# Softmax over rows of 512: one in-place ring, the row maximum, and small chunks at both ends

## Chip, cores, metric

The kernel runs on one core of one Trainium2 chip. The metric is device time in microseconds (us) of one execution. Before: 163.57 us, median of 3 runs (163.49 to 163.68).

## The reference

```python
x = np.random.randn(16, 1024, 512).astype(np.float32)

def reference(x):
    x_max = np.max(x, axis=-1, keepdims=True)
    exp_x = np.exp(x - x_max)
    return (exp_x / np.sum(exp_x, axis=-1, keepdims=True)).astype(np.float32)
```

There are 16384 rows of 512 numbers, 33.55 MB in and 33.55 MB out. Spread over 128 partitions, that is 128 rows of 2 KB for each partition. In what follows "a row" means one row in every partition: 128 rows must be loaded and 128 stored.

## The kernel before

Sixteen chunks of 8 rows. Loads go out from SyncE's queue, stores from ScalarE's (ACT's). Input and output have separate tiles. The maximum is off: with numbers drawn from a normal distribution the exponentials do not overflow.

```python
R, XBUFS, EBUFS = 8, 7, 4
for t in range(nchunks):                                   # 16
    x_tile = x_pool.tile([P, R, d], F32)                   # 7 buffers
    nc.sync.dma_start(out=x_tile, in_=x_t[t])
    nc.gpsimd.tensor_copy(out=guard_tile, in_=x_tile[:, 0, 0:1])
    # ... use_max is off: no reduce_max ...
    e_tile = e_pool.tile([P, R, d], F32)                   # 4 buffers
    for r in range(R):
        nc.scalar.activation(out=e_tile[:, r, :], in_=x_tile[:, r, :], func=Exp,
                             bias=0.0, scale=1.0, accum_out=sums[:, r : r + 1])
    nc.vector.reciprocal(out=recip, in_=sums)
    nc.vector.tensor_mul(out=e_tile, in0=e_tile, in1=recip_b)   # 128x4096, recip broadcast
    nc.scalar.dma_start(out=out_t[t], in_=e_tile)
# ... four memsets on GpSimd at the end ...
```

The softmax here doesn't subtract the row's maximum and nothing guards it: scores larger than these inputs give would overflow.

Of the kernel before, what the change touches and what calls it, by code (L numbers as in the profile page):

```python
# [2 lines left out]

# [4 lines left out]


@with_exitstack  # L10
def kernel(
    ctx: ExitStack,
    tc: tile.TileContext,
    x: bass.AP,
    out: bass.AP,
):
    nc = tc.nc
    P = nc.NUM_PARTITIONS

    x_flat = x.flatten_outer_dims()  # L20
    out_flat = out.flatten_outer_dims()
    n, d = x_flat.shape

    R = int(os.environ.get("SM_R", "8"))
    XBUFS = int(os.environ.get("SM_XBUFS", "7"))
    EBUFS = int(os.environ.get("SM_EBUFS", "4"))

    rows_per_chunk = P * R
    assert n % rows_per_chunk == 0
    nchunks = n // rows_per_chunk  # L30

    x_t = x_flat.rearrange("(t p r) d -> t p r d", p=P, r=R)
    out_t = out_flat.rearrange("(t p r) d -> t p r d", p=P, r=R)

    x_pool = ctx.enter_context(tc.tile_pool(name="xp", bufs=XBUFS))
    e_pool = ctx.enter_context(tc.tile_pool(name="ep", bufs=EBUFS))
    stats_pool = ctx.enter_context(tc.tile_pool(name="stats", bufs=12))
    guard_pool = ctx.enter_context(tc.tile_pool(name="guard", bufs=1))

    use_max = os.environ.get("SM_USEMAX", "0") == "1"  # L40

    guard_tile = guard_pool.tile([P, 1], mybir.dt.float32)

    e_tiles = []
    for t in range(nchunks):
        x_tile = x_pool.tile([P, R, d], mybir.dt.float32)
        nc.sync.dma_start(out=x_tile, in_=x_t[t])  # L47

        nc.gpsimd.tensor_copy(out=guard_tile, in_=x_tile[:, 0, 0:1])  # L49

        if use_max:
            neg_max = stats_pool.tile([P, R], mybir.dt.float32)
            nc.vector.reduce_max(
                out=neg_max, in_=x_tile, axis=mybir.AxisListType.X, negate=True
            )

        e_tile = e_pool.tile([P, R, d], mybir.dt.float32)
        e_tiles.append(e_tile)
        sums = stats_pool.tile([P, R], mybir.dt.float32)
        for r in range(R):  # L60
            nc.scalar.activation(  # L61
                out=e_tile[:, r, :],
                in_=x_tile[:, r, :],
                func=mybir.ActivationFunctionType.Exp,
                bias=neg_max[:, r : r + 1] if use_max else 0.0,
                scale=1.0,
                accum_out=sums[:, r : r + 1],
            )

        recip = stats_pool.tile([P, R], mybir.dt.float32)  # L70
        nc.vector.reciprocal(out=recip, in_=sums)  # L71

        recip_b = recip.unsqueeze(2).to_broadcast([P, R, d])
        nc.vector.tensor_mul(out=e_tile, in0=e_tile, in1=recip_b)  # L74

        nc.scalar.dma_start(out=out_t[t], in_=e_tile)  # L76

    for b in range(min(EBUFS, nchunks)):
        e_tile = e_tiles[nchunks - 1 - b]
        nc.gpsimd.memset(e_tile[:, 0, 0:1], 0.0)  # L80


# [1 line left out]
_INS = ['x']  # L84
_OUTS = [((16, 1024, 512), 'float32')]


# [23 lines left out]
```

## Time and profile before

| | before |
|---|---|
| median | 163.57 us |
| span of the profiled run | 161.6 us |
| DVE (VectorE) busy | 74.0 us |
| ACT (ScalarE) busy | 80.8 us |
| transfers | 67.1 MB, 415 GB/s over the span |

These lines are from the page of the kernel before. The rows of 40 digits cut the span into 40 equal slices (4.0 us each); a digit is the busy share of its slice in tenths, 9 being 90% or more. A costliest-group line reads: line, engine, operation, output from input, shapes, count, then busy us and mean ns of one, then idle time just before. POOL is GpSimd.

```profile
span 161.6 us, 456 instructions
...
DVE 74.0 (46%) x32; ACT 80.8 (50%) x257; POOL 18.5 (11%) x24
...
DVE  0006970994196419082000008941992499069600
ACT  3089519924893481900000199339906970995000
...
DMA  5999999999999999999999999999999999999993
GB/s 150 434 434 426 434 373 422 432 430 430 438 426 426 446 422 426 450 422 426 446 410 442 438 418 438 434 422 440 426 430 442 418 434 442 418 434 442 418 434 146
...
L61 ACT ACTIVATE e_tile<-x_tile 128x512 f32<-128x512 f32 x128 | 78.5, 615 | 66.1 <-DMA x_tile<-in_x_dram 35.1
L74 DVE TENSOR_TENSOR e_tile<-e_tile,recip 128x4096 f32<-128x4096 f32 x16 | 70.8, 4425 | 0.5
```

The DMA row is the one to read first: nine in every slice but the first and the last. No engine is busy for more than half of the span. So the kernel is bound by its transfers, and it can only gain where the row is not 9.

The same as a table of stretches (start and end in us, length, busy us of each engine with its count, clock, DMA share, GB/s):

```profile
core 0: us, DVE busy (x) ACT busy (x) POOL busy (x), PEclk, DMA share, GB/s
...
30.00:100.00 70.00, 28.92 (x13) 31.09 (x101) 9.92 (x8) 1.00 1.01 431
...
112.00:140.00 28.00, 18.51 (x8) 17.69 (x57) 4.82 (x3) 1.00 1.01 430
140.00:161.00 21.00, 9.25 (x4) 7.57 (x26) 0.40 (x4) 1.00 0.91 389
```

The Trainium skill, "DMA: Bandwidth & Descriptors", section "Where 436 GB/s comes from", gives 16 ports of 32 bytes at 850 MHz as the ceiling, 435 GB/s. The trace agrees: 431 and 430 GB/s over long stretches (single slices swing to both sides of that).

The last links of the chain that ended last (start us, length us, what):

```profile
147.84 4.43 DVE e_tile L74
...
152.35 8.28 DMA out_dram<-e_tile
```

A store of 2 MB alone takes 4.9 us at this rate. This one took 8.28 us from issue to landing, because one more store was still ahead of it.

### The profile page before, as it was taken

Reading aid. Unit: us, or ns where it says so; the run is one execution under the profiler, and the core shown is the slowest. Engines: PE = TensorE matmul, PEld = TensorE weight load, DVE = VectorE, ACT = ScalarE, POOL = GpSimd, SP = SyncE. Lnnn points to the kernel's source line nnn. Section 1 sums busy time; section 2 is a strip of 40 time slices with the busy share of each in tenths; the row PEclk is TensorE's granted clock in tenths of the full one; section 3 lists DMA queues with packets and bytes.
Section 4 is the critical chain, followed back from the end, with each engine's and each line's share of the span. In section 5 each row is a group of like instructions: output and inputs, shape, how many; then the busy total and the mean of one; then the engine's idle time right before and its main releaser. Section 6 shows DMA issues by size and latency. Waiting matters only on the chain.

```text
span 161.6 us, 456 instructions
## 1 busy us (share of the span) xinstructions
DVE 74.0 (46%) x32; ACT 80.8 (50%) x257; POOL 18.5 (11%) x24
## 2 busy tenths in 40 slices
DVE  0006970994196419082000008941992499069600
ACT  3089519924893481900000199339906970995000
POOL 0000000034090001000000006200082000000000
DMA  5999999999999999999999999999999999999993
GB/s 150 434 434 426 434 373 422 432 430 430 438 426 426 446 422 426 450 422 426 446 410 442 438 418 438 434 422 440 426 430 442 418 434 442 418 434 442 418 434 146
DMA packets 4610, 67.13 MB, mean 415 GB/s; under 512 B 512, under 2 KB 512, under 8 KB 512
## 3 DMA queue, kind: packets, MB, share of 16 engines
q1 hardware_dynamic: 2304, 33.56, 49.4%
q10 hardware_dynamic: 2304, 33.56, 48.5%
q14 instruction: 2, 0.02, 0.0%
HBM read 33.55 MB, written 33.55 MB: 415 GB/s over the span
## 4 chain that ended last, share of the span: by engine, by line
DMA 52%; ACT 28%; DVE 17%; issue 1%; ACTq 1%; POOLq 0%; SPq 0%
DMA x_tile<-in_x_dram 35%; ACT e_tile L61 28%; DMA out_dram<-e_tile 17%; DVE e_tile L74 16%; DVE recip L71 1%; ACTq L76 1%; POOLq L106 0%; POOLq L80 0%; SPq L47 0%
## 5 line engine op out<-in xcount | busy, mean ns | idle before, releaser
L61 ACT ACTIVATE e_tile<-x_tile 128x512 f32<-128x512 f32 x128 | 78.5, 615 | 66.1 <-DMA x_tile<-in_x_dram 35.1
L74 DVE TENSOR_TENSOR e_tile<-e_tile,recip 128x4096 f32<-128x4096 f32 x16 | 70.8, 4425 | 0.5
L71 DVE RECIPROCAL recip<-sums 128x8 f32<-128x8 f32 x16 | 3.2, 203 | 77.7 <-ACT e_tile L61 77.7
L49 POOL COPY guard_tile<-x_tile 128x1 f32<-128x1 f32 x16 | 17.9, 1116 | 119.0 <-DMA x_tile<-in_x_dram 119.0
L61 ACT ACTIVATION_READ_ACCUMULATOR e_tile<-x_tile 128x1 f32 x128 | 23.9, 187 | 0.0
L80 POOL MEMSET e_tile<- 128x1 f32 x4 | 0.4, 99 | 23.1 <-DMA out_dram<-e_tile 23.1
L61 ACT ACT_TABLE_LOAD x1 | 1.3, 1283 | 0.7 <-PEq L95 0.7
L95 POOL MEMSET const-float32-0.0<- 128x1 f32 x1 | 0.1, 99 | 0.2 <-issue 0.2
L95 POOL MEMSET const-uint8-127<- 128x1 uint8 x1 | 0.1, 103 | 0.0
L95 POOL MEMSET const-bfloat16-1.0<- 128x1 bf16 x1 | 0.1, 102 | 0.0
L95 POOL MEMSET const-float32-1.0<- 128x1 f32 x1 | 0.1, 99 | 0.0
## 6 DMA issues: line engine op xcount, KB each, us to landing
x_tile<-in_x_dram SPq DMA_DIRECT2D x16, 2048.0 KB, 42.2
out_dram<-e_tile ACTq DMA_DIRECT2D x16, 2048.0 KB, 18.2
```

What stands on the lines that cost most here:

```text
L49: nc.gpsimd.tensor_copy(out=guard_tile, in_=x_tile[:, 0, 0:1])
L61: nc.scalar.activation(out=e_tile[:, r, :], in_=x_tile[:, r, :], func=mybir.ActivationFunctionType.Exp, bias=neg_max[:, r : r + 1] if use_ ...
L71: nc.vector.reciprocal(out=recip, in_=sums)
L74: nc.vector.tensor_mul(out=e_tile, in0=e_tile, in1=recip_b)
L76: nc.scalar.dma_start(out=out_t[t], in_=e_tile)
L80: nc.gpsimd.memset(e_tile[:, 0, 0:1], 0.0)
L95: nc = _bacc.Bacc("TRN2", target_bir_lowering=False, num_devices=1)
```

## The change

It does four things at once: it adds the row maximum; it computes in place, in one ring of eleven 8-row buffers; it multiplies row by row with a per-partition scalar; and it makes the first and the last chunks small, so that compute starts earlier and the last chain is short. (GpSimd's guard copies and its last memsets go too.) The core of it:

```diff
+CHUNKS = [1, 1, 2, 4] + [8] * 14 + [4, 2, 1, 1]
+SLOTS = {1: 2, 2: 1, 4: 1, 8: 11}
 # ... (views by chunk, pools: cut)
+    def load(k):
+        tiles[k] = data.tile([P, R, d], F32, name=f"x{R}", tag=f"x{R}", bufs=SLOTS[R])
+        nc.sync.dma_start(out=tiles[k], in_=src[k])
+    def rowmax(k):
+        nc.vector.reduce_max(out=shift[k], in_=tiles[k], axis=AX, negate=True)
+    def exps(k):
-                out=e_tile[:, r, :],
-                in_=x_tile[:, r, :],
+                out=tiles[k][:, r, :],
+                in_=tiles[k][:, r, :],
-                bias=neg_max[:, r : r + 1] if use_max else 0.0,
+                bias=shift[k][:, r : r + 1],
+    def scale(k):
-        nc.vector.tensor_mul(out=e_tile, in0=e_tile, in1=recip_b)
+        for r in range(R):
+            nc.vector.tensor_scalar_mul(out=tiles[k][:, r, :], in0=tiles[k][:, r, :],
+                                        scalar1=recip[:, r : r + 1])
+    def store(k):
+        nc.scalar.dma_start(out=dst[k], in_=tiles[k])
+    with tc.manual_schedule():
+        for k in range(K):
+            load(k); rowmax(k); exps(k)
+            if k >= 1:
+                scale(k - 1); store(k - 1)
+        scale(K - 1); store(K - 1)
```

The store of chunk k-1 stands on ACT's queue behind the exponentials of chunk k. Chunks are counted from 0 below, so chunks 4 to 17 have 8 rows.

## The prediction

> **What bounds it now.** The transfers. The page shows the DMA engines at nine tenths or more in 38 of 40 slices, at 410 to 450 GB/s; DVE is busy 46% and ACT 50%. The windows view gives 432 GB/s for 30-96 us and 413 for 136-160. The Trainium skill, "DMA: Bandwidth & Descriptors", section "Where 436 GB/s comes from", puts the ceiling at 435 GB/s; this trace agrees (434 at best). 67.1 MB at 430 GB/s are 156 us of the 161.6 us span. The chain of waits names ACT and DVE for long stretches (28% and 17%), but they only kept pace with the queues: the last store was issued at 152.35 us and landed 8.28 us later, though 2 MB need 4.9, so stores were queued to the end.
>
> **What the change does.** No byte is saved. Nothing large can be won.
> - Maximum: DVE gains one reduction over every element. The multiply of 128x4096 takes 4425 ns today; the skill's "VectorE: DVE Perf Modes", section "The perf-mode tier table", has tensor_reduce at 1x like the fp32 tensor_tensor, so I estimate 4.4 us per 8 rows. It gives fp32 tensor_scalar 2x: 8 operations of about 0.33 to 0.42 us, 2.6 to 3.4 us in place of 4.4. With the reciprocal an 8-row chunk costs DVE some 7.3 to 8.1 us, 117 to 131 us in all. Below the 9.7 us that loading and storing a chunk take together, but above the 4.9 us of storing alone.
> - ACT: the same 128 exps of 613 ns, now in place, about 79 us; POOL's guards go.
> - Small end chunks start compute near 4 us instead of 8.5 and shorten the last chain, but DMA is already full in both places. 32 transfers become 44, a few with 2 KB pieces: estimate 0 to 1 us.
> - The ring is ample, yet in the listing of the built kernel the transfers still share eight completion semaphores. The store of the twelfth chunk waits until the load five chunks later has landed, and the next waits for the load after that. They stand on ACT's queue, so exps stop too. Loads then run alone for about 15 us and several stores are left for the end, where DVE's 7.3 to 8.1 us per chunk is slower than the stores' 4.9. I estimate 1 to 4 us of DMA idle near 140-155 us.
>
> **Sum.** 156.7 us of packets + 2.1 before the first + 1 slow first packets + about 2 idle near the end + about 1 small pieces = 162.8 us span; the measured time lies 2 us above the span: **164.8 us**. Range 162.4 to 167.8. Chances: faster by over 2%: 3%; within 2%: 82%; slower by over 2%: 15%.
>
> **What would show the steps right or wrong.** DMA still full from about 3 to 140 us, DVE busy 110 to 135 us, ACT near 80. Reductions of 128x4096 near 4.4 us; 128x512 multiplies at 0.33 to 0.42 us apart. One ACT gap of about 10 to 15 us near 95-110 us, ended by a load's landing, a DMA slice below nine tenths near 140-155 us.
>
> **What would make it wrong.** If the multiplies run at 1x (0.6 us), a chunk costs DVE 9.4 us, and the end becomes bound by DVE: 168 us or more. If the shared semaphores are free when reached, no stall: 162 to 163. If 2 KB pieces move slowly, 1 to 3 us more.

## The result

| | before | after |
|---|---|---|
| median | 163.62 us (4 runs, 163.49 to 163.79) | 165.82 us (4 runs, 165.38 to 167.05) |
| span of the profiled run | 161.6 us | 164.1 us |
| DVE busy | 74.0 us | 125.8 us |
| ACT busy | 80.8 us | 93.7 us |

The ratio is 1.0148, with a 95% interval of 1.0111 to 1.0185: slower by 1.5%, within 2%. Ratios here are the mean time of one kernel's fast runs over the mean of the other's in the same rounds, so they are not quite the ratio of the quoted medians. Repeated on another occasion (below), the change took 166.21 us against 163.67.

The page of the kernel after:

```profile
span 164.1 us, 559 instructions
...
DVE 125.8 (77%) x172; ACT 93.7 (57%) x257; POOL 0.2 (0%) x4
...
DVE  1774999999996986959599595800099999999940
ACT  2544399595959294582918500004995959597520
...
DMA  5999999999999999999999999999999999968996
GB/s 164 371 413 419 425 438 426 423 431 439 431 405 447 435 427 415 447 435 427 415 447 435 421 423 443 431 427 419 447 404 458 416 421 438 414 276 379 383 396 243
...
L63 ACT ACTIVATE x<-x,shift 128x512 f32<-128x512 f32 x128 | 90.6, 708 | 60.5 <-DVE shift L57 24.3
L57 DVE TENSOR_REDUCE shift<-x 128x8 f32<-128x4096 f32 (+3 forms) x22 | 71.6, 3253 | 17.5 <-DMA x<-in_x_dram 17.4
L77 DVE TENSOR_SCALAR x<-x,recip 128x512 f32<-128x512 f32 x128 | 52.7, 482 | 0.8
```

In the DMA row, the 36th slice and its neighbours are no longer full: 6 and then 8, with 276 GB/s where the kernel before moves 434. In the ACT row there are 0s in slices 24 to 27, where the DMA row is still all nines. The stretches (columns as before):

```profile
30.00:100.00 70.00, 60.58 (x80) 41.18 (x116) 0.00 (x0) 1.00 1.01 432
100.00:112.00 12.00, 4.42 (x1) 0.00 (x0) 0.00 (x0) 1.00 1.00 427
112.00:140.00 28.00, 21.02 (x30) 22.72 (x63) 0.00 (x0) 1.00 1.01 427
140.00:164.00 24.00, 17.43 (x35) 12.00 (x34) 0.00 (x0) 1.00 0.84 350
```

Between 100 and 112 us ACT does nothing at all and the transfers lose nothing. From 140 us on they do: share 0.84 and 350 GB/s to the end of the span, against 0.91 and 389.

The timeline of the gap (start us, length us, engine, line, operation, count, and in brackets the idle time before and what ended it):

```profile
86.74 3.26 DVE L77 TENSOR_SCALAR x<-x,recip 128x512 f32<-128x512 f32 x8
...
101.59 4.42 DVE L57 TENSOR_REDUCE shift<-x 128x8 f32<-128x4096 f32 x1 [1.82 <-DMA x<-in_x_dram]
112.63 0.34 ACTq L84 DMA_DIRECT2D out_dram<-x  x1
113.09 0.72 ACT L63 ACTIVATE x<-x,shift 128x512 f32<-128x512 f32 x1 [20.66 <-DMA x<-in_x_dram]
...
118.87 0.20 DVE L75 RECIPROCAL recip<-sums 128x8 f32<-128x8 f32 x1 [12.86 <-ACT x L63]
```

DVE finished chunk 11's multiplies at 90.0 us (86.74 + 3.26), and ACT had done the exponentials that stand before the store at 92.4 (113.09 - 20.66). The store left only at 112.63: it was held 20.2 us. ACT's next exponential waited 20.66 us, and the trace names a load as what ended it; DVE, for its part, waited 12.86 us for the exponentials that followed.

The end of the same timeline, reductions and stores only:

```profile
130.01 4.42 DVE L57 TENSOR_REDUCE shift<-x 128x8 f32<-128x4096 f32 x1
130.14 0.34 ACTq L84 DMA_DIRECT2D out_dram<-x  x1
...
137.75 4.41 DVE L57 TENSOR_REDUCE shift<-x 128x8 f32<-128x4096 f32 x1
137.87 0.34 ACTq L84 DMA_DIRECT2D out_dram<-x  x1
...
145.48 2.28 DVE L57 TENSOR_REDUCE shift<-x 128x4 f32<-128x2048 f32 x1
145.60 0.34 ACTq L84 DMA_DIRECT2D out_dram<-x  x1
...
151.57 0.34 ACTq L84 DMA_DIRECT2D out_dram<-x  x1
```

The reductions stand 7.74 us apart and so do the stores, while a store of 2 MB occupies the engines for 4.9 us. That is DVE's pace of a chunk: 4.4 us reduction, 0.2 reciprocal, 3.3 us of multiplies.

To put a number on the loss I counted, from the packet records, how many of the 16 DMA engines stood without a packet at each moment between the first and the last packet (16 less the packets under way), summed this over time, and divided by 16:

| | first to last packet | idle, first 20 us | idle from 140 us after the first packet on |
|---|---|---|---|
| before | 158.6 us | 0.3 us | 1.1 us |
| after | 160.9 us | 0.3 us | 2.5 us |

The kernel before has its 1.1 us because the engines do not finish together: in its last 1.5 us, on average, about five of the 16 still had a packet. The change has 1.4 us more, and has it elsewhere: only 0.1 us lies in its last microsecond, and 2.4 us lie in two holes, 144 to 147 us and 151 to 153 us. The 8-row stores of these times left at 145.60 and 151.57 us, as soon as DVE was done with them.

### The profile page after: what moved, and what is told of

It is laid out like the page before. It is cut to its first block, busy times and chain, and to the rows that moved or that the text cites. A ratio compares the mean times of both kernels' runs of the same rounds, so it can differ in the third digit from the quotient of the medians.

```text
span 164.1 us, 559 instructions
## 1 busy us (share of the span) xinstructions
DVE 125.8 (77%) x172; ACT 93.7 (57%) x257; POOL 0.2 (0%) x4
## 5 line engine op out<-in xcount | busy, mean ns | idle before, releaser
L63 ACT ACTIVATE x<-x,shift 128x512 f32<-128x512 f32 x128 | 90.6, 708 | 60.5 <-DVE shift L57 24.3
L57 DVE TENSOR_REDUCE shift<-x 128x8 f32<-128x4096 f32 (+3 forms) x22 | 71.6, 3253 | 17.5 <-DMA x<-in_x_dram 17.4
L77 DVE TENSOR_SCALAR x<-x,recip 128x512 f32<-128x512 f32 x128 | 52.7, 482 | 0.8
L63 ACT ACTIVATION_READ_ACCUMULATOR x<-x,shift 128x1 f32 x128 | 23.9, 187 | 0.0
L75 DVE RECIPROCAL recip<-sums 128x8 f32<-128x8 f32 (+3 forms) x22 | 4.0, 182 | 14.1 <-ACT x L63 14.1
## 6 DMA issues: line engine op xcount, KB each, us to landing
out_dram<-x ACTq DMA_DIRECT2D x2, 512.0 KB, 10.4
```

The costliest lines, as they stand in the source:

```text
L57: nc.vector.reduce_max(out=shift[k], in_=tiles[k], axis=AX, negate=True)
L63: nc.scalar.activation(out=tiles[k][:, r, :], in_=tiles[k][:, r, :], func=EXP, bias=shift[k][:, r : r + 1], scale=1.0, accum_out=sums[k][: ...
L75: nc.vector.reciprocal(out=recip, in_=sums[k])
L77: nc.vector.tensor_scalar_mul(out=tiles[k][:, r, :], in0=tiles[k][:, r, :], scalar1=recip[:, r : r + 1],)
```

## The experiments

Eleven runs were made: ten new kernels and, once more, the change.

**Theories.** A: the stores are held back. The transfers of this kernel signal their end on eight semaphores, handed out in turn to loads and stores together, and a transfer waits until the one that had its semaphore before it has landed. The listing of the built kernel shows for the change:

```
store of chunk 11 waits for the load of chunk 16
store of chunk 12 waits for the load of chunk 17
store of chunk 14 waits for the load of chunk 18
... 15 for 19, 16 for 20, 17 for 21
```

The semaphore records of the profiled run agree: the load of chunk 16 landed at 112.56 us and the store of chunk 11 left at 112.63; the load of chunk 17 landed at 118.66 and the store of chunk 12 left at 118.74. The kernel before has such a tie too: its store of chunk 7 left at 92.07 us, when the load of chunk 10 had landed (91.97), and ACT had waited 23.4 us. There it cost nothing (from its list of waits: us in total, times, longest):

```profile
ACT e_tile L61 <- DMA x_tile<-in_x_dram: 35.1, 4, 23.4
```

The loads of the last small chunks have buffers of their own, so the scheduler lists them early, and by the listing they shift the turns, so that later stores get semaphores which loads still hold (no run tested this alone). ACT stops at such a store, and what DVE then has left, at 7.7 us a chunk, is more than the stores can hide. B: the maximum makes DVE too slow wherever the waits stand. C: small pieces and more transfers cost it (a piece is what a transfer moves for one partition: 2 KB in a chunk of 1 row, 16 KB in a chunk of 8).

### e1_ring5: five 8-row buffers

```diff
-SLOTS = {1: 2, 2: 1, 4: 1, 8: 11}
+SLOTS = {1: 2, 2: 1, 4: 1, 8: 5}
```

> Only the number of 8-row buffers goes from 11 to 5, so loads cannot be listed far ahead of stores and the listing has the stores of the eighth-last chunk and later no longer wait for loads that are still to come (only one store, that of chunk 14, waits for the load two chunks later). Theory A (stores held back by shared completion semaphores, then an end at DVE's pace of 7.7 us a chunk): no ACT gap near 100-112 us, no idle of the transfers near 142-152 us, 163.0 to 164.2 us. Theory B (the row maximum makes DVE too slow wherever the waits stand): stays at 165.3 to 166.3. Theory C (small pieces and extra transfers cost it): stays at 165.3 to 166.3. If five buffers are too few, loads starve early, DMA slices below nine tenths before 100 us, and it is slower than 166.

Measured: 164.47 us (164.21 to 164.94), ratio 1.0055 (1.0041 to 1.0069). Page and waits (waiter, waited for, us in total, times, longest us):

```profile
DMA  4999999999999999999999999999999999999994
GB/s 165 314 423 425 438 427 426 437 423 431 427 437 423 427 435 431 419 431 439 419 427 439 431 429 431 435 423 431 439 423 439 431 419 428 441 411 432 437 401 161
```

```profile
ACT x L63 <- DVE shift L57: 28.6, 11, 7.8
ACT x L63 <- issue: 28.5, 8, 4.1
```

No wait of ACT for a load is left among the long ones, and the DMA row is full to the end; idle from 140 us on is 0.85 us, no more than in the kernel before. So A holds for about 1.35 us of the 2.2 (1.7 of 2.5 by the repeat below). But the time lies above what A expected: 0.9 us are unexplained by it. The first 20 us now show 1.05 us idle against 0.3.

### e2_nomax: eleven buffers, no maximum

```diff
-                bias=shift[k][:, r : r + 1],
+                bias=0.0,
 ...
-            rowmax(k)
```

> The reduction goes and the bias is the constant 0.0; ring, chunks and buffers stay, and the listing still has the stores of chunks 11 and 13 wait for the loads of 16 and 17. Results stay right for this input. Theory A: the ACT gap of some 10 us stays, but after it a chunk costs DVE 3.4 us and ACT about 4.9 to 5.7, close to a store's 4.9, so little or no idle at the end: 163.2 to 164.6. Theory B: 163.2 to 164.0, and no gap matters. Theory C: 165.3 to 166.3. Side question: an exp with constant bias should be back at 613 ns from 706.

Measured: 164.61 us (164.03 to 164.93), ratio 1.0056 (1.0041 to 1.0071), at the very top of A's range (0.01 us above it) and clearly below C's; results right.

```profile
DMA  5999999999999999999999999999999999999993
...
L63 ACT ACTIVATE x<-x 128x512 f32<-128x512 f32 x128 | 78.6, 615 | 63.0 <-DMA x<-in_x_dram 60.2
```

```profile
ACT x L63 <- DMA x<-in_x_dram: 60.2, 13, 24.6
```

The gap is even longer, 24.6 us, and yet the DMA row has no hole: idle from 140 us on is 1.2 us, as good as before. With 3.3 us of DVE work a chunk, the end keeps up. So a gap alone costs nothing here. And the exponential is back at 615 ns from 708. The Trainium skill, "ScalarE: Activation LUTs", section "What ACT_TABLE_LOAD costs", has each [128,1] pointer operand add about 93 ns; the trace agrees, 706 against 613 ns at the median.

### e3_uniform: sixteen chunks of 8 rows

```diff
-CHUNKS = [1, 1, 2, 4] + [8] * 14 + [4, 2, 1, 1]
+CHUNKS = [8] * 16
```

> Sixteen chunks of 8 rows, everything else as after the change (ring of 11, maximum). Compute starts at 8.5 us, not 3.2, so DVE at 7.7 us a chunk stays behind the loads almost to the end and the shared semaphores should be free when stores reach them. Theory A: no long ACT gap that a load ends, stores queued to the end, 162.6 to 164.0. Theory B: 165 or more. Theory C: 162.6 to 164.0 as well, with or without a gap.

Measured: 163.21 us (163.1 to 163.33), ratio 0.9976 (0.9964 to 0.9988): faster than the kernel before, with the maximum, in place, by a quarter of a per cent. It too has a gap (ACT waited 11.8 us for a load, between 75.8 and 87.7 us), which I had not expected, and it cost nothing. The timeline shows why: its last three stores were issued early enough.

```profile
135.69 0.34 ACTq L84 DMA_DIRECT2D out_dram<-x  x1
...
143.42 0.34 ACTq L84 DMA_DIRECT2D out_dram<-x  x1
...
149.39 0.34 ACTq L84 DMA_DIRECT2D out_dram<-x  x1
```

The last store left at 149.39 us, and the engines, still busy with the ones ahead, came to it at about 154.3. In the change the last store leaves at 158.24.

### e4_before_max: the maximum in the kernel before

```diff
-    use_max = os.environ.get("SM_USEMAX", "0") == "1"
+    use_max = os.environ.get("SM_USEMAX", "1") == "1"
```

> The kernel before with its own switch for the maximum turned on: separate output tiles, uniform chunks, multiply of 128x4096. DVE then needs 4.4 + 0.2 + 4.4 = 9.1 us a chunk, 146 us in all, against 9.7 us of transfers. Theory B in its strongest form (maximum alone costs the 2 us): 165.5 to 167. Theory A: DVE is so near the transfers' pace that the end is exposed by a chunk: 165 to 169. A result within 163.0 to 164.2 would tell against any cost of the maximum by itself.

Measured: 179.98 us, ratio 1.0996 (1.098 to 1.1012), far slower than I expected.

```profile
DVE  0189899999994689999999999997993279667810
...
DMA  6999999999999999999999999998259609686974
```

DVE is full through most of the span and the DMA row breaks up from the 28th slice on. DVE was busy 142.4 us and idle some 28 us, so it ended near 170 us. I had left those waits out of the sum; a pace of 9.1 us a chunk hardly wins them back against 9.7 us of transfers. That reading is argued from this one run, not tested further; ACT too stood still three times, for 8 to 20 us, and what began these waits was not traced. The run suggests that the maximum needs the cheaper multiplies: in the change a chunk costs DVE 7.7 us, and there the maximum can be hidden entirely (e3, e5).

### e5_ring5_fours: no piece under 8 KB, five buffers

```diff
-CHUNKS = [1, 1, 2, 4] + [8] * 14 + [4, 2, 1, 1]
-SLOTS = {1: 2, 2: 1, 4: 1, 8: 11}
+CHUNKS = [4, 4] + [8] * 14 + [4, 4]
+SLOTS = {1: 2, 2: 1, 4: 2, 8: 5}
```

> The version with five 8-row buffers, and the small chunks 1, 1, 2, 4 and 4, 2, 1, 1 drawn together to 4, 4 at each end: no piece under 8 KB, 36 transfers in place of 44. If the 0.9 us that the five-buffer version still stands above the kernel before are small pieces and gaps between the first short loads (theory C, now as the second term): 163.2 to 163.9, and in the first 20 us the transfers idle about as little as before. If those 0.9 us belong to the maximum, the in-place ring or the five buffers: stays at 164.2 to 164.8.

Measured: 163.17 us (163.09 to 163.53), ratio 0.9983 (0.9972 to 0.9995). Against e1 that is 1.3 us less by the medians. In the profiled runs, idle in the first 20 us is 0.5 us against 1.05, and idle at the end 0.55 against 0.85. So C holds for the rest, and with these ends the maximum, the ring and the five buffers cost nothing.

### e6_pieces2k: every piece 2 KB

```diff
 # chunks [8] * 16
-            views.append(part.rearrange("(p r) d -> p r d", r=R))
+            views.append(part.rearrange("(r p) d -> p r d", r=R))
```

> The uniform kernel with only the rows of a chunk laid out the other way: each partition takes every 128th row, so every transfer is cut into pieces of 2 KB, same bytes, same instructions. If a 2 KB piece costs 84 ns wherever it stands, against 76.4 ns for an eighth of a 16 KB piece of 611 ns, the 2048 pieces per engine cost 15.6 us more: 177 to 181 us. The change has only 64 such pieces per engine, and 32 each of 4 and 8 KB, so it pays about 0.8 us of it. If small pieces are slow only in the first microseconds, when the queues are being filled, this stays within 163 to 166.

Measured: 173.65 us, ratio 1.0627 (1.0603 to 1.065). Slower throughout, so small pieces are not slow only at the start, but by less than I had worked out.

```profile
DMA  4999999999999999999999999999999999999995
...
DMA packets 33283, 67.14 MB, mean 392 GB/s; under 512 B 512, under 2 KB 512, under 8 KB 33280
```

The trace gives 84 ns a piece at the median, as expected; but neighbouring pieces overlap. From e3 to e6 the time grew by 10.4 us for 1792 more pieces per engine: 5.8 ns each. The change has 96 more pieces per engine than the kernel before, so about 0.6 us by this measure. (The new layout also changes the order of addresses; this run does not tell the two apart.)

### e7_ring7: seven buffers

```diff
-SLOTS = {1: 2, 2: 1, 4: 1, 8: 11}
+SLOTS = {1: 2, 2: 1, 4: 1, 8: 7}
```

> As after the change with seven 8-row buffers: the listing has the store of chunk 12 wait for the load of chunk 16, and that of chunk 14 for the load of 17, so the stores are held later and for a shorter time than with eleven. Theory A: an ACT gap of some 5 to 10 us about ten us later than with eleven, idle of the transfers near the end between the two, 164.3 to 165.8 us. If the gap is not the cause: the same time as with eleven or as with five, whatever the gap.

Measured: 164.65 us (164.22 to 165.65), ratio 1.0074 (1.0051 to 1.0097). The gap is there (ACT waited 14.5 us for a load, until 119.2 us). The time is between e1 and the change, but its interval overlaps that of e1, so it does not tell five from seven. In its profiled run, the slowest of six (165.65 us), the idle from 140 us on is 1.55 us, between that of e1 (0.85) and that of the change (2.5).

### e8_big16: pieces of 32 KB in the middle

```diff
-CHUNKS = [1, 1, 2, 4] + [8] * 14 + [4, 2, 1, 1]
-SLOTS = {1: 2, 2: 1, 4: 1, 8: 11}
+CHUNKS = [8] + [16] * 6 + [8, 8, 4, 4]
+SLOTS = {16: 5, 8: 1, 4: 2}
 ...
+        B = 16 if 1 <= k <= 8 else R
+        whole = data.tile([P, B, d], F32, name=f"x{B}", tag=f"x{B}", bufs=SLOTS[B])
+        tiles[k] = whole[:, :R, :]
```

> A version meant to be faster, with the maximum kept: chunks of 8, six of 16, then 8, 8, 4, 4 rows, five large buffers, so three quarters of the bytes move in pieces of 32 KB and no store waits for a late load. If a piece costs a fixed 9 ns beside its bytes, as 84, 159, 309 and 611 ns for 2, 4, 8 and 16 KB suggest, a 32 KB piece takes about 1213 ns and the transfers save 0.6 us: 162.2 to 163.2. If the larger chunk makes the buffers wait (a load needs a store that comes later), DMA idles in the middle and it is slower than 164.

Measured: 164.01 us (163.92 to 165.33), ratio 1.0053 (1.0026 to 1.008). A miss. A 32 KB piece did take 1213 ns at the median, but on average 1239 ns in loads and 1224 in stores, so the 0.6 us did not appear. Idle at the end was 1.1 us, as in the kernel before. Where the rest went I did not settle.

### e9_after_again, e10_ring5_nomax, e11_ring11_fours: one chip, three kernels

e9 is the change itself.

> The change itself once more, on the chip of the next two runs, so that the differences of about 1 us are read on common ground: 165.3 to 166.5 us, some 2.2 us above the kernel before, with the ACT gap near 100 to 112 us and idle transfers near 142 to 152 us.

Measured: 166.21 us (165.55 to 167.49), ratio 1.0169 (1.0136 to 1.0202; "unclear" by the rule of 2%, as the interval reaches over it). The hole is in the same slices:

```profile
DMA  5999999999999999999999999999999999969996
```

e10 takes away the maximum (the diff of e2) and has five buffers (the diff of e1).

> Both taken away: five 8-row buffers (no store waits for a far load) and no maximum. It fills the fourth corner beside eleven buffers with the maximum (165.8), eleven without (164.6) and five with (164.5). If the end needs both the late gap and the slow DVE, this corner is no faster than the other two: 164.1 to 164.9. If each costs about 1.2 us by itself, it comes to 163.0 to 163.6.

Measured: 164.55 us (164.03 to 165.78), ratio 1.0063 (1.0034 to 1.0092). The four corners, as ratios to the kernel before:

| | with the maximum | without |
|---|---|---|
| eleven buffers (late gap) | 1.0148 and 1.0169 | 1.0056 |
| five buffers (no gap) | 1.0055 | 1.0063 |

Three corners are alike and one stands out, so the loss at the end needs both: the late gap and the slower DVE. That neither costs anything by itself is shown by e1 and e2, whose DMA rows have no hole. The fourth corner is less clean than its number: in its profiled run (165.14 us, 0.6 above its median) the last load of 1 row was done at 158.2 us (150.1 in e1), the last store left at 160.03, and the transfers idled 1.6 us from 140 us on. It has a loss of its own, of another origin, so the table alone does not rule out that the two costs add.

e11 puts eleven buffers back under the 4, 4 ends.

```diff
 CHUNKS = [4, 4] + [8] * 14 + [4, 4]
-SLOTS = {1: 2, 2: 1, 4: 2, 8: 5}
+SLOTS = {1: 2, 2: 1, 4: 2, 8: 11}
```

> The 4, 4 ends with eleven buffers again. The listing now has the store of the ninth chunk wait for the load four chunks later, so the ACT gap comes back, but some 15 us earlier than in the change (ending near 96 us, not 112). If a gap by itself costs a microsecond: 164.2 to 165. If only the time at which DVE then gets done counts (estimate: about 53 us of DVE work after the gap, done near 149 us, well before the transfers end near 160): no idle at the end, 163.0 to 163.6, as with five buffers.

Measured: 163.74 us (163.6 to 163.83), ratio 1.0003 (0.9991 to 1.0016), 0.14 us above the range that I gave to "only the time at which DVE gets done counts" and below that of "a gap by itself costs". Its timeline around the gap, and its page:

```profile
97.43 0.34 ACTq L84 DMA_DIRECT2D out_dram<-x  x1
97.89 0.72 ACT L63 ACTIVATE x<-x,shift 128x512 f32<-128x512 f32 x1 [14.04 <-DMA x<-in_x_dram]
```

```profile
DVE  0589999999599595977959690399999999996400
...
DMA  5999999999999999999999999999999999999994
```

With the maximum and with a gap of 14.04 us, but ending at 97.9 us and not at 113, DVE is done at 151.1 us and the DMA row stays full; idle from 140 us on is 0.7 us. The gap is harmless here. That this is because DVE gets done early enough fits the profiles: DVE's last instruction ends at 158.2 us in the change, 156.6 in e7, 155.0 in e1 and 151.1 here, and the idle from 140 us on is 2.5, 1.55, 0.85 and 0.7. When the gap ends does not decide it alone: that of e7 ends later (119.2) than that of the change (113.1), with less work left. The ends differ between e11 and the change too, so this run alone does not separate them; and no run took away the shared semaphores and kept all else.

## Why the prediction was right, and where it was off

- *Bound by transfers, so nothing large can be won.* Right. The two fastest versions (e3, e5) are 0.2% below the kernel before.
- *The shared semaphores hold the store of the twelfth chunk until a load five chunks later; loads then run alone; several stores are left for the end; 1 to 4 us of idle near 140 to 155 us.* Right: the hold is shown by the landing times, its cost by e1 and e2; e7 and e11 fit. The store of chunk 11 was held 20.2 us (92.4 to 112.6), the DMA row has its hole after it, in slices 36 and 37, and the idle from 140 us on is 2.5 us, where I had put "about 2". The length of the ACT gap was off: 20.7 us, not 10 to 15. It did not matter, as the loss comes from the work left after the gap.
- *DVE 7.3 to 8.1 us a chunk.* Right: 7.74 us; reduction 4412 ns, multiplies 481 ns long and 0.40 us apart. The Trainium skill, "VectorE: DVE Perf Modes", section "The perf-mode tier table", has fp32 tensor_scalar at 2x and tensor_reduce at 1x. The trace agrees: the reduction takes as long as the multiply of two tensors did (4425 ns), the scalar multiplies less.
- *ACT: the same 128 exps of 613 ns.* Wrong: 706 ns, for the bias is now a pointer. It cost 12 us of ACT's time, off the critical path, as ACT had 60 us of idle.
- *Small pieces 0 to 1 us.* Right at the upper end: 0.9 us between e1 and the kernel before (1.3 between e1 and e5, where no piece is under 8 KB), in two parts: idle gaps between the first short loads and about 0.6 us of pieces (e6). How the idle divides between start and end was not tried apart, since the start varies from run to run (0.3 to 1.1 us in the profiles of kernels with these ends).
- *Sum 162.8 us span, 164.8 us.* Measured 164.1 us and 165.82. The sum stopped at the last packet, and there it was good: the last packet of the change ended at 162.7 us. It left out the time from there to the end of the span, which the kernel before shows too: 1.4 us in the change, 1.3 us before (160.3 to 161.6). That term is the miss.

## What to carry to other kernels

When the transfers are full, a long gap of an engine may be harmless and a short one costly: ask whether the work left after the gap, at the pace of the slowest engine, still ends before the queued stores do. Look in the listing for waits that the program does not ask for: buffers that let loads be listed far ahead can tie a store to a load that is still far from landing. Very small chunks pay only where they fill a hole that the profile shows; here there was none at either end, and chunks of 4 or 8 rows were better.

## What the Trainium skill lacked or had wrong

- No page says that transfers sharing a few completion semaphores can hold a store until a later load lands; "DMA: Bandwidth & Descriptors" only asks for one semaphore for each transfer in flight. Here it held a store 20.2 us and stopped ACT for 20.7.
- "DMA: Bandwidth & Descriptors", section "Where 436 GB/s comes from", says that for transfers between HBM and SBUF the HBM share of about 358 GB/s binds. With one core running, the kernels before and after held 427 to 433 GB/s over stretches of 12 to 70 us. The sentence does not hold for a core that runs alone; the same section has 425 GB/s for one large transfer.
- The same page gives rates by size of a whole transfer, for software-made descriptors. What a piece costs on the queues of SyncE and ACT is not there: 84, 159, 309, 611 and 1213 ns for 2, 4, 8, 16 and 32 KB, and, with overlap, 5.8 ns for each piece more.
- The same page, section "Queues, rings and completion order", says that an engine alternates between queues by packets of typically 9 to 17 descriptors, but not what follows when the pieces differ in size. Here the turns look like single pieces: the load of 1 row in 2 KB pieces (chunk 20, 8 for each engine) took from 129.5 to 135.0 us (at the middle of the 16 engines) beside stores in 16 KB pieces, about 8 turns of 84 + 611 ns.
- "VectorE: DVE Perf Modes", in its errata table, has 58 cycles beside the elements, which would make 0.33 us for 512 fp32 numbers at 2x (the page itself says that this row is too low for one operation); the multiplies here start 0.40 us apart.
